# Keeping TensorE's instructions in source order inside the attention heads of a hybrid attention, SSD and retention network

## The chip, the cores and the metric

The kernel runs on one core of one Trainium2 chip. The metric is the device time of one execution in microseconds, and lower is better.

## The reference

Two layers transform 1024 latent tokens and 256 context tokens of width 1024. Each layer normalises the tokens, projects them with one wide matrix, and feeds three mixers that run side by side: differential attention with 4 heads, a bidirectional state-space scan with 16 heads, and bidirectional retention with 4 heads. Their gated outputs are joined and projected back. In the last layer the context tokens serve only as keys and values and as starting states. The part that the change touches is the attention:

```python
def diff_attention(q, k, v, lam):
    s = jnp.einsum('bqhmd,bkhmd->bhmqk', q, k).astype(jnp.float32) * (ATT_QK_DIM ** -0.5)
    p = jax.nn.softmax(s, axis=-1)
    a = p[:, :, 0] - lam * p[:, :, 1]
    return jnp.einsum('bhqk,bkhe->bqhe', a.astype(v.dtype), v)
...
    attn_lat = attn_out(diff_attention_blocked(q_l, jnp.concatenate([k_l, k_c], axis=1),
                                               jnp.concatenate([v_l, v_c], axis=1), lam), ag)
```

Every head has two score maps (m = 0 and 1). The second one's softmax, times lambda, is taken from the first one's, and the difference meets the values. A latent query block of 128 rows sees all 1280 keys; a context query block (first layer only) sees the 256 context keys.

## The kernel before, in words

All dense products are made of three matmuls each, on a split of both factors into a high and a low part (`mm3`, lines 301 to 312). A dense group is 24 such matmuls into one PSUM buffer: L310 with 512 or 256 moving columns (`t_group`: the gates and the output projection), L312 with 256 (`dense_n`, used by `two_units`: queries, keys and values). PSUM has 2 buffers for dense groups (`mm`), 3 for scores (`s`), 2 for transposes (`t`) and 1 for outputs (`o`). Work tiles of SBUF share 8 buffers.

The source is a set of Python generators. `phase(mixer, budget)` walks a mixer, here `head_loop`, step by step; after each step the mixer yields how far it is, and `phase` calls `pump` for dense groups of the stream `dense_all` until the dense work issued reaches that share of the budget. A `two_units` group counts 2.6 and a gates group 5.12 (2.56 with 256 columns). For the heads the budgets are 65, 52, 65, 65 in the first layer and 46, 46, 59, 45 in the second (`SHARE`, line 40, entries 9 to 12). So the source fixes a place for each dense group between steps of a head.

One pass i of `head_loop` (line 1045) in source order is:
- `head_b(i, 0)` (line 979): scores of map 0 of block i, six matmuls (L986) into three `s` buffers, 512, 512 and 256 keys wide; the maximum of each (DVE, L988), their joint maximum `nb` (DVE, L993), and three exponentials with sums (ACT, L998), which give the `s` buffers back
- `head_c1(i-1)`: sums and the factor `rho` of the block before, then `e0 + rho*e1` over 1280 columns (DVE, L1016); first place for dense groups
- `head_c2(i-1)` (line 1020): ten transposes (L149) of that result into three `t` buffers, four, four and two, each copied to SBUF as `aT` (L116 on ACT and L118 on DVE by turns); then `head_a(i+2)` (line 970): four transposes of the split queries `qhl` into one more `t` buffer, copied as `qT`; second place
- `head_b(i, 1)`: scores of map 1, as above; third place
- `head_c3(i-1)` (line 1032): ten products of `aT` with the values (L1037, two matmul records each); then at times one step of `finish_head` of the head before (transposes of `O`) or of `head_prep` of the next one (ten transposes of split keys `khl` for each map); fourth place

The last line of the program that matters here is `TileContext(nc, schedule_with_timeline_sim=True)`. It means that the order of each engine's instructions is not the source's: a planner lays them out before the kernel is run, on a simulated clock. An engine that is free takes, of the instructions that are ready by that clock, the earliest in the source. On the chip every engine then issues its instructions in that fixed order.

Of the kernel before, what the change touches and what calls it, by code (L numbers as in the profile page):

```python
# [47 lines left out]
def drain(g):  # L48
    for _ in g:
        pass  # L50


class Net:
    def __init__(self, tc, ctx, a, outs):
        self.tc, self.nc, self.a, self.outs = tc, tc.nc, a, outs
        ep = ctx.enter_context
        self.act_p = ep(tc.tile_pool(name="act", bufs=1))
        self.w_p = ep(tc.tile_pool(name="wgt", bufs=2))
        self.u_p = ep(tc.tile_pool(name="unit", bufs=NU))
        self.s_p = ep(tc.tile_pool(name="work", bufs=NW))  # L60
        self.c_p = ep(tc.tile_pool(name="const", bufs=1))
        self.t_p = ep(tc.tile_pool(name="tiny", bufs=2))
        self.d_p = ep(tc.tile_pool(name="dram", bufs=1, space=DRAM))
        self.ps_mm = ep(tc.tile_pool(name="ps_mm", bufs=2, space=PSUM))
        self.ps_s = ep(tc.tile_pool(name="ps_s", bufs=3, space=PSUM))
        self.ps_t = ep(tc.tile_pool(name="ps_t", bufs=2, space=PSUM))
        self.ps_o = ep(tc.tile_pool(name="ps_o", bufs=1, space=PSUM))
        self.uid = 0
        self.flip = 0
        self.queue = []  # L70
        self.ready = []
        self.have = {}
        self.ydone = {}
        self.later = []
        self.pieces = []
        self.wu = []
        self.alive = False
        self.x1k = {}
# [1295 lines left out]
    def layer(self, l):  # L1374
        last = l == DEPTH - 1
        cols, cv = self.cc_[l]
        self.mix = self.d_p.tile([16, P, TOK], F32, tag=f"mix{l}", name=f"mix{l}")
        self.x1 = self.d_p.tile([KT, P, TOK], F32, tag=f"x1_{l}", name=f"x1_{l}")
        xin = self.a["xt"] if l == 0 else self.xl
        self.have, self.ydone, self.grp, self.pair, self.heads = {}, {}, {}, {}, {}  # L1380
        self.mixed = False
        self.x1t = {}

        def chain(*gs):
            for i, g in enumerate(gs):
                for f in g:
                    yield (i + (f if f is not None else 0.5)) / len(gs)

        self.first_dense(l, cv, last, self.posts, self.pre)
        self.stream = self.dense_all(l, last, cols, cv, xin)  # L1390
        self.alive = True
        self.phase(chain(self.dt_rest, self.bc_prep(0, last), self.pair_prep(0),
                         self.decay_bufs(), self.g_prep(0, last)), 26)
        share = SHARE[l]
        prep = self.head_prep(0, last)
        for p in range(8):
            def extra(p=p):
                if p == 3:
                    yield from self.bc_prep(1, last)
                    yield from (None for _ in range(4))  # L1400
                if p < 7:
                    yield from self.pair_prep(p + 1)
                else:
                    for _ in range(1):
                        yield next(prep)
            self.phase(self.pair_phase(p, cols, last, extra()), share[p])
        self.post = iter(())
        self.phase(chain(prep), share[8])
        for h in range(4):
            ex = self.head_prep(h + 1, last) if h < 3 else ()  # L1410
            self.phase(self.head_loop(h, last, ex), share[9 + h])
        self.phase(self.ret_mix(0, last), share[13])
        self.phase(self.ret_mix(1, last), share[14])
        drain(self.post)
        self.mixed = True
        while self.alive or self.later:
            self.pump()
        xout = self.outs
        if not last:
            self.xl = xout = self.d_p.tile([KT, P, TOK], F32, tag="xl", name="xl")  # L1420
        self.out2(l, last, cols, xout)
# [132 lines left out]
```

## Time and profile before

| what | value |
|---|---|
| median of 3 runs | 2871.17 us (2867.28 to 2872.06) |
| the profiled execution | 2869.1 us |
| its span, first to last instruction | 2867.3 us |
| TensorE (PE) busy | 2665.5 us, 93% of the span |
| VectorE (DVE) busy | 1781.3 us, 62% |
| ScalarE (ACT) busy | 1056.4 us, 37% |
| mean granted TensorE clock | 0.964 of full speed |

The time of a run is that of the program on the device; the span leaves out 1.8 us before the first and after the last instruction. TensorE has a row for matmuls (PE) and one for weight loads (PEld) that overlaps it. The ends of matmuls are modelled, so that PE counts as busy for some 0.16 us after the last matmul of a chain has been issued and passed.

### The profile page before, as it was taken

The page shows a single profiled execution, that of the slowest core. Times are in us where ns is not written, and L with a number is a line of the kernel's source. Part 1 is how long each engine was busy: PE and PEld are TensorE (multiplying, and loading weights), DVE is VectorE, ACT ScalarE, POOL GpSimd, SP SyncE. Part 2 cuts the span into 40 slices and gives each one's busy share as a digit, 9 for nine tenths or more (in the row PEclk, how much of TensorE's full clock was granted, in tenths as well). Part 3 has the DMA queues.
Part 4 walks back from the last instruction along what each step waited for, and adds up shares of the span by engine and source line. Part 5 has one row for each costly group of instructions (what it writes and reads, how often), then busy time and mean ns, then how long its engine had stood idle before and what let it go on. Part 6 is the DMA issues. An engine that isn't in the chain of part 4 may idle for free.

```text
span 2867.3 us, 45100 instructions
## 1 busy us (share of the span) xinstructions
PE 2665.5 (93%) x17116; PEld 2339.0 (82%) x17116; DVE 1781.3 (62%) x4213; ACT 1056.4 (37%) x2678; POOL 772.1 (27%) x688
## 2 busy tenths in 40 slices
PE   6799999999999999989989989999999999999999
PEld 4578877888888899977878777878988888889787
DVE  5567767656677766565435566667676767564651
ACT  3443333224454545341223443332254444442330
POOL 2333223232111121243331423223421221022540
PEclk9899999999999999998999999999999999999999
DMA  6021212222111111033452112112210010002461
GB/s 244 10 62 62 67 44 83 70 69 89 45 54 45 54 31 39 27 110 109 136 179 95 36 41 72 53 50 65 60 30 16 23 30 23 23 17 66 139 209 55
DMA packets 111832, 196.04 MB, mean 68 GB/s; under 512 B 13600, under 2 KB 43104, under 8 KB 111616
## 3 DMA queue, kind: packets, MB, share of 16 engines
q1 hardware_dynamic: 111616, 193.17, 21.3%
q8 instruction: 135, 2.21, 0.3%
q14 instruction: 81, 0.66, 0.1%
HBM read 155.43 MB, written 37.68 MB: 67 GB/s over the span
## 4 chain that ended last, share of the span: by engine, by line
PE 76%; DVE 12%; ACT 3%; issue 2%; DMA 2%; POOL 1%; SPq 0%; DVEq 0%; ACTq 0%; POOLq 0%
PE mm L310 34%; PE mm L312 18%; PE t L149 5%; PE o L1037 4%; PE s L986 4%; PE s L772 2%; PE s L822 2%; DVE mx L988 2%; PE o L815 2%; PE t L793 1%; ACT e L998 1%; DVE e L1016 1%; DMA mr<-mix 1%; DVE rs L1156 1%; PE s L1146 1%
## 5 line engine op out<-in xcount | busy, mean ns | idle before, releaser
L310 PE MATMUL mm<-ah,wh 128*128 128x512 f32 (+1 forms) x1680 | 629.4, 375 | 30.1 <-DVE xr L1223 13.8
L310 PE MATMUL mm<-al,wh 128*128 128x512 f32 (+1 forms) x1680 | 622.8, 371 | 1.5 <-DVE al L284 0.9
L310 PE MATMUL mm<-ah,wl 128*128 128x512 f32 (+1 forms) x1680 | 622.4, 371 | 0.6 <-POOL wl L284 0.6
L284 POOL TENSOR_TENSOR wl<-raw,wh 128x512 fp32r<-128x512 f32 x224 | 294.5, 1335 | 769.5 <-ACT wh L282 736.9
L312 PE MATMUL mm<-wh,ah 128*128 128x256 f32 x1568 | 455.7, 291 | 9.5 <-DVE q L118 7.0
L312 PE MATMUL mm<-wl,ah 128*128 128x256 f32 x1568 | 450.4, 287 | 0.0
L312 PE MATMUL mm<-wh,al 128*128 128x256 f32 x1568 | 448.7, 286 | 0.0
L310 PEld LDWEIGHTS mm<-ah,wh 128*128 128x128 f32 x1680 | 322.3, 192 | 85.8 <-issue 13.8
L310 PEld LDWEIGHTS mm<-al,wh 128*128 128x128 f32 x1680 | 322.2, 192 | 51.1 <-issue 1.4
L310 PEld LDWEIGHTS mm<-ah,wl 128*128 128x128 f32 x1680 | 321.2, 191 | 51.2 <-POOL wl L284 1.1
L312 PEld LDWEIGHTS mm<-wh,ah 128*128 128x128 f32 x1568 | 302.5, 193 | 16.6 <-DVE q L118 7.7
L998 ACT ACTIVATE e<-s,nb 128x512 f32<-128x512 f32 (+1 forms) x384 | 231.7, 613 | 206.2 <-DVE nb L993 203.6
L312 PEld LDWEIGHTS mm<-wl,ah 128*128 128x128 f32 x1568 | 302.7, 193 | 2.4 <-POOL wl L284 0.2
L312 PEld LDWEIGHTS mm<-wh,al 128*128 128x128 f32 x1568 | 302.3, 193 | 2.2 <-issue 0.2
L988 DVE TENSOR_REDUCE mx<-s 128x1 f32<-128x512 f32 (+1 forms) x400 | 225.1, 589 | 55.4 <-PE s L986 53.2
L986 PE MATMUL s<-kT,qT 128*128 128x512 f32 (+1 forms) x800 | 215.8, 375 | 17.0 <-ACT e L998 15.5
L282 ACT ACTIVATE wh<-raw 128x512 fp32r<-128x512 f32 x224 | 130.0, 625 | 226.2 <-PE mm L310 103.9
L1037 PE MATMUL o<-v,aT 128*128 128x128 f32 x1312 | 174.9, 276 | 0.0
L986 PEld LDWEIGHTS s<-kT,qT 128*128 128x128 f32 x800 | 134.3, 193 | 41.3 <-ACT e L998 26.5
L1037 PEld LDWEIGHTS o<-v,aT 128*128 128x128 f32 x1312 | 163.8, 193 | 4.1 <-DVE v L118 0.8
L794 ACT ACTIVATE t<-t 128x512 f32<-128x512 f32 x144 | 82.2, 582 | 146.5 <-PE t L793 142.5
L766 POOL TENSOR_TENSOR xw<-xn,dtpk 128x512 f32<-128x512 f32 (+2 forms) x96 | 79.4, 838 | 208.9 <-PE s L772 93.5
(282 smaller groups left out, 4544.5 us busy)
## 6 DMA issues: line engine op xcount, KB each, us to landing
raw<-in_wi_dram SPq DMA_DIRECT2D x176, 256.0 KB
wa<-in_wa_dram SPq DMA_DIRECT2D x48, 512.0 KB
E<-cume SPq DMA_DIRECT2D x144, 128.0 KB
mr<-mix SPq DMA_DIRECT2D x64, 256.0 KB
raw<-in_wo_dram SPq DMA_DIRECT2D x32, 256.0 KB
x<-xr SPq DMA_DIRECT2D x26, 256.0 KB
mix<-cv SPq DMA_DIRECT2D x8, 640.0 KB
mix<-sg SPq DMA_DIRECT2D x8, 640.0 KB
```

The lines of the kernel that those rows point to most:

```text
L149: self.nc.tensor.transpose(ps[:, j * P:(j + 1) * P], srcs[i + j], self.ident)
L282: nc.scalar.activation(out=hi, in_=x, func=AF.Copy)
L284: e.tensor_tensor(out=lo, in0=x, in1=hi.bitcast(F32), op=ALU.subtract)
L310: nc.tensor.matmul(ps, lhsT=w, rhs=x, start=st, stop=sp)
L312: nc.tensor.matmul(ps, lhsT=x, rhs=w, start=st, stop=sp)
L766: nc.gpsimd.tensor_tensor(out=xw, in0=xn[:, a:a + m].rearrange("p t (h e) -> p t h e", h=2), in1=self.wend[:, a:a + m, h0:h0 + 2].unsqueez ...
L772: nc.tensor.matmul(ps[:, j * P:(j + 1) * P], lhsT=bn[:, c, :], rhs=xw[:, j].rearrange("p h e -> p (h e)"), start=True, stop=True)
L794: nc.scalar.activation(out=ps, in_=ps, func=AF.Exp)
L986: nc.tensor.matmul(ps[:, 0:n], lhsT=qT[:, 2 * m + s, :], rhs=kT[m][:, t0:t0 + n], start=(s == 0), stop=(s == 1))
L988: nc.vector.tensor_reduce(out=mx[:, ci:ci + 1], in_=ps[:, 0:n], axis=AX.X, op=ALU.max, negate=len(chunks) == 1)
L998: nc.scalar.activation(out=em[:, t0:t0 + n], in_=pss[ci][:, 0:n], func=AF.Exp, bias=nb, accum_out=z[:, 3 * m + ci:3 * m + ci + 1])
L1037: nc.tensor.matmul(po[:, 0:P], lhsT=aT[j], rhs=v[:, j, :], start=(j == b0), stop=(j == NT - 1))
```

## The change

A thin wrapper `Ordered` stands in front of TensorE. While its flag `pin` is set, each matmul or transpose that is traced gets an edge that keeps it, in the planner's order, behind the instruction traced just before it on TensorE. The edge sets the order of issue and no wait. The flag is set in `layer` around the four `head_loop` phases, with all the dense groups that `phase` pumps into them. `Core` passes the other engines through as they were.

```diff
+class Ordered:
+
+    def __init__(self, tc, tensor):
+        self.tc, self.tensor, self.pin = tc, tensor, False
+
+    def kept(self, ins):
+        if self.pin:
+            self.tc.keep_in_program_order(ins)
+        return ins
+
+    def matmul(self, *a, **k):
+        return self.kept(self.tensor.matmul(*a, **k))
+
+    def transpose(self, *a, **k):
+        return self.kept(self.tensor.transpose(*a, **k))
+
+
+class Core:
+    def __init__(self, tc):
+        self.tensor = Ordered(tc, tc.nc.tensor)
+        for x in ("vector", "scalar", "gpsimd", "sync"):
+            setattr(self, x, getattr(tc.nc, x))
...
-        self.tc, self.nc, self.a, self.outs = tc, tc.nc, a, outs
+        self.tc, self.nc, self.a, self.outs = tc, Core(tc), a, outs
...
             ex = self.head_prep(h + 1, last) if h < 3 else ()
+            self.nc.tensor.pin = True
             self.phase(self.head_loop(h, last, ex), share[9 + h])
+            self.nc.tensor.pin = False
```

## Rows read from the trace of the kernel before

**Rows 1.** The page, busy time of each engine over the span.
```profile
PE 2665.5 (93%) x17116; PEld 2339.0 (82%) x17116; DVE 1781.3 (62%) x4213; ACT 1056.4 (37%) x2678; POOL 772.1 (27%) x688
```

**Rows 2.** Busy time in the head stretches of both layers; then clock, DMA share.
```profile
635.00:1180.00 545.00, 520.20 (x3789) 471.79 (x3789) 373.76 (x895) 253.40 (x773) 97.67 (x64) 0.99 0.15 47
2085.00:2580.00 495.00, 458.77 (x3263) 422.31 (x3262) 342.08 (x812) 229.24 (x691) 93.17 (x66) 0.98 0.08 24
```

**Rows 3.** What TensorE waited for, 635 to 1180: total us, times, longest.
```profile
PE s L986 <- ACT e L998: 7.6, 7, 2.2
PE t L149 <- DVE khl L284: 6.1, 5, 2.7
```

**Rows 4.** The same, 2085 to 2580.
```profile
PE s L986 <- ACT e L998: 7.9, 8, 2.2
PE t L149 <- DVE khl L284: 5.0, 5, 2.9
```

**Rows 5.** Timeline of TensorE from 641.5: start, us, engine, line, operation.
```profile
641.64 0.63 PE L986 MATMUL s<-kT,qT 128*128 128x512 f32 x2
642.11 0.28 PE L312 MATMUL mm<-wh,ah 128*128 128x256 f32 x1
...
642.57 0.62 PE L986 MATMUL s<-kT,qT 128*128 128x512 f32 x2
```

**Rows 6.** Timeline of TensorE from 2361; idle before and its releaser in brackets.
```profile
2362.52 1.06 PE L149 MATMUL t<-ident,e 128*128 128x128 f32 x8 [0.50 <-DVE e L1016]
2364.33 0.44 PE L149 MATMUL t<-ident,e 128*128 128x128 f32 x2 [0.75 <-ACT aT L116]
2367.19 0.45 PE L149 MATMUL t<-ident,qhl 128*128 128x128 f32 x1 [2.43 <-DVE nb L993]
...
2379.69 1.82 PE L986 MATMUL s<-kT,qT 128*128 128x512 f32 x4 [2.19 <-ACT e L998]
```

**Rows 7.** Windows of 10 us around it; the clock follows POOL.
```profile
2350.00:2360.00 10.00, 10.00 (x78) 9.54 (x78) 5.99 (x13) 7.03 (x21) 6.51 (x6) 1.00 0.32 87
2360.00:2370.00 10.00, 6.32 (x41) 5.71 (x41) 7.77 (x14) 2.81 (x8) 1.02 (x1) 0.84 0.07 19
```

**Rows 8.** Timeline from 853, all engines.
```profile
853.50 1.07 PE L149 MATMUL t<-ident,khl 128*128 128x128 f32 x8 [2.74 <-DVE khl L284]
...
854.17 0.60 ACT L116 ACTIVATE kT<-t 128x512 fp32r<-128x512 f32 x1 [1.31 <-PE t L149]
854.61 0.69 DVE L118 CAST kT<-t 128x512 fp32r<-128x512 f32 x1 [0.65 <-PE t L149]
...
854.82 0.69 PE L149 MATMUL t<-ident,khl 128*128 128x128 f32 x2 [0.25 <-ACT kT L116]
...
855.35 1.12 PE L149 MATMUL t<-ident,e 128*128 128x128 f32 x4
```

**Rows 9.** Groups by line, 635 to 1180: count, busy us, mean ns of one.
```profile
L988 DVE TENSOR_REDUCE mx<-s 128x1 f32<-128x512 f32 (+1 forms) x208 | 116.0, 583 | 30.5 <-PE s L986 29.3 <-ACT e L998 0.3
L1016 DVE SCALAR_TENSOR_TENSOR e<-e,rho,e 128x1280 f32<-128x1280 f32 (+1 forms) x40 | 57.6, 1441 | 0.8
L993 DVE TENSOR_REDUCE nb<-mx 128x1 f32<-128x3 f32 x64 | 9.8, 153 | 0.9
L998 ACT ACTIVATE e<-s,nb 128x512 f32<-128x512 f32 (+1 forms) x192 | 115.8, 613 | 106.1 <-DVE nb L993 103.8 <-PE t L149 1.9
L998 ACT ACTIVATION_READ_ACCUMULATOR e<-s,nb 128x1 f32 x192 | 38.6, 201 | 0.0
```

**Rows 10.** Long pieces of the chain that ended last: start, us, what.
```profile
104.44 11.10 PE mm L310 x48
...
2443.55 8.63 PE mm L312 x72
```

**Rows 11.** Timeline of TensorE from 858.2.
```profile
858.94 2.40 PE L1037 MATMUL o<-v,aT 128*128 128x128 f32 x20
...
861.99 0.94 PE L986 MATMUL s<-kT,qT 128*128 128x512 f32 x4
```

## The prediction

> **What bounds the kernel now.** I read the page first, for the engine that sets the end. TensorE is busy for 93% of the span, VectorE for 62% [rows 1], so the end moves with the time in which TensorE waits or runs slowly. Next come the windows of the two head stretches, 1040 us together. TensorE is busy for 520.2 and 458.8 us of them and idle for 61.0 us, VectorE is busy for 69% and ScalarE for 46%, and the granted clock is 0.99 and 0.98 [rows 2]. [...]
>
> Then the list of waits in each stretch tells what ends those idle times: 15.5 us of scores that wait for exponentials to free a score buffer, and 11.1 us of key transposes that wait for the split `khl` [rows 3, 4]. The rest is spread over many short waits. The timeline shows how the planner's order works. Where dense work is at hand, a pair of scores stands between single matmuls of a dense group [rows 5]: each step of a head comes just when the planner thinks that its input is ready, and dense matmuls fill what is between. Where the planner placed no dense work, TensorE stops between the steps of a head, for 2.43 and 2.19 us [rows 6], and the clock falls to 0.84 in that window of 10 us, after 1.00 in the one before [rows 7].
>
> **The change, part by part.** No operation is added or dropped; the wrapper is gone by the time the program runs. What changes is TensorE's order in the heads, and, by the planner's clock, the orders that VectorE, ScalarE and GpSimd take behind it. In source order the six scores of a map stand together, so do the fourteen transposes of `head_c2` and `head_a`, the twenty products, and each dense group. So three things move.
>
> *Waits that go away.* The key transposes keep their place behind the products of a block and their splits; I leave their 11.1 us as they are. That leaves 61 - 11 = 50 us of idle that belongs to the planner's order. A wait is longer than the view shows, since a matmul of 256 columns is shown as 0.28 us long [rows 5] while 72 of them follow each other in 8.63 us, 0.12 each [rows 10]: the last 0.16 us before a wait count as busy. The four kinds of rows 3 and 4 make 26.6 us in 25 waits, 1.06 us each; at that mean the 50 us are some 47 waits, and 47 x 0.16 is 8. I take away 58 us.
>
> *A wait that comes with the source order.* The transposes have two buffers. Source order asks for 4, 4, 2 and again 4 transposes without anything between. The trace has one such run, 4, 4 and 2 of `khl` and then 4 of `e` [rows 8]: TensorE starts at 853.50, ScalarE's copy of the first buffer ends at 854.77, the third group starts at 854.82, VectorE's copy of the second ends at 855.30, and the fourth starts at 855.35. These 1.85 us hold ten transposes, which take 0.114 us each ((1.07 - 0.16) / 8 in the same rows), so 1.14; 0.71 us is lost. Without the fourth group it is 1.32 - 8 x 0.114 = 0.41. Today the planner mostly puts dense matmuls or scores into these gaps; the pinned order can't. There are 64 blocks with all keys (8 in each of 4 heads and 2 layers), and 48 of them have a `head_a` behind (7 per head in the first layer, where ten blocks run, 5 in the second). That makes 48 x 0.71 + 16 x 0.41 = 41 us. Both copies ran there as soon as they could. That is the lower bound; the upper one is the run where the third group waited for a visible 0.75 us after eight transposes [rows 6], three times the 0.25 of rows 8, about 0.5 more for each block, 73 us. A copy finds VectorE busy in 69% of cases, with half an operation of 0.4 us to go, and ScalarE in 46%, and few other things compete at that point, so I stay near the lower bound and add 0.1 us for each block: 47 us.
>
> *Chains that source order leaves too little room for.* From the start of a map's scores a chain runs to the first free score buffer: 0.62 for two scores [rows 5], three maxima at 0.58, `nb` 0.15, one exponential with its sum 0.61 + 0.20: 3.3 us. All three exponentials end at 4.95 us, and with three tiny steps (taken like `nb`) and the combination at 1.44 the transposes can begin at 6.85 us [rows 9]. Against that stands the work that source order puts between. A dense group takes 24 x 0.12 = 2.9 us with 256 columns, 24 x 0.23 = 5.55 with 512 [rows 10]; six scores at these rates 1.2, the products 2.4 [rows 11], fourteen transposes 1.6. A pass of the first layer gets 65 / 11 = 5.9 of its budget, two groups of 2.6 or about one of 5.12, so most passes have dense work in two of their four places: 1.2 + 2.9 + 2.4 + 1.2 + 2.9 = 10.6 us between the scores of map 1 and the transposes that need them, and 3.75 to spare. I walked the loop with its budgets through both layers. Between the scores of the two maps nine places have no dense group and 2.8 us (0.5 short each, 4.5 in all), and once two sets of scores stand side by side (2.1 short); between the scores of map 1 and the transposes ten places have less than 6.85 (2.4 once, 5.2 twice, 5.9, 6.5 twice, 6.7 three times, and one just met; 10 us short). The sum is 16.5 us. A TensorE that waits for one of them gives room to the next, down to 5 us in all; one more us of queue in front of VectorE lifts it to 41. I take 20, as VectorE has free time in 31% of the stretch. At the start of each of eight heads, scores follow two groups of query transposes and wait for a copy of about 0.7 us: 6 us (bounds 3 and 8).
>
> *Sum.* New waits 47 + 20 + 6 = 73, less 58: 15 us longer. The profiled execution took 2869.1 us, 2.1 below the median of the runs shown, so 2884 there and 2886 as a median. The bounds: 41 + 5 + 3 - 58 = -9 and 73 + 41 + 8 - 58 = +64 us.
>
> TensorE's queue holds everything behind a waiting instruction, so a wait for a copy also holds back the next scores and, one step on, VectorE's maxima. No DMA is moved past another by the pins, which act on TensorE alone; a dense group that runs later asks for its weights later, and GpSimd, which splits them, is busy for 18% of the stretch [rows 2].
>
> On the clock, the stretch after the long waits had 0.84 [rows 7]. [...]
>
> **The rivals.** *Faster: slack beats the planner's timing.* The planner leaves a head's step no time to spare, and pays where its clock is wrong or its dense work has been spent, as in rows 6. Source order spreads dense groups evenly and leaves 3 to 4 us in most chains. [...] It decides when less than about 0.8 us for each block is lost in all. Against it speaks that 41 of today's 58 us come back for certain, by two buffers.
>
> *Nothing to measure.* The same terms cancel: 58 out, 52 to 64 in. 2871. By the sum, 15 us decide between this and the forecast, less than the bounds of one term.
>
> *Much slower: queues in front of VectorE.* If VectorE's planned order doesn't suit and each copy and each chain meets a queue, the terms are at their upper bounds: +45 to +64 us, 2925. Against it: it has 31% free time.
>
> [...]
>
> **How the numbers follow.** Forecast (+6 to +45) 0.40, faster 0.30, no change 0.18, much slower by queues 0.08 and by the clock 0.04. A measurement can tell 0.2%, 5.7 us, from no change. So faster 0.30, same 0.18, slower 0.52. The range from 2842 to 2926 leaves out the far ends of the first and the last two cases, about 0.07 below and 0.10 above; it holds both signs. The forecast's own range is 2877 to 2916.
>
> **What would show it.** In the profile after: six scores, twenty products and fourteen transposes each in one piece; transposes of `e` and `qhl` that wait for `aT` copies, for 0.25 us and more, in most blocks (new: some 15 to 30 us in the list of waits); scores that wait for exponentials only where no dense group stands between; no clusters of 2 us without dense work; the clock at 0.98 or above. The prediction is wrong if waits for `aT` stay under 10 us in all, if the idle time of the two stretches falls below 45 us, or if the time moves outside the heads.

## The result, and the profile after

The changed kernel takes 3045.43 us (median of 4 runs, 3039.06 to 3047.56), against 2870.86 for the kernel before beside it. The ratio is 1.0608, with a 95% interval from 1.059 to 1.0625. It is 175 us slower. The forecast was 15 us longer, and the range ended at 2926.

The page of the changed kernel, span and busy time of each engine [rows 1]:
```profile
span 3041.5 us, 45101 instructions
...
PE 2731.6 (90%) x17116; PEld 2370.8 (78%) x17116; DVE 1789.0 (59%) x4213; ACT 1068.6 (35%) x2678; POOL 767.4 (25%) x688
```
The instruction counts are the same on every engine. TensorE's busy time has grown by 66 us with the same 17116 matmuls, so part of the loss isn't waiting. The windows of its two head stretches, in the columns of [rows 2]:
```profile
630.00:1286.00 656.00, 567.74 (x3830) 499.44 (x3830) 372.18 (x886) 259.00 (x770) 94.08 (x64) 0.93 0.12 39
2193.00:2734.00 541.00, 469.10 (x3140) 420.17 (x3141) 339.68 (x788) 230.67 (x683) 89.02 (x63) 0.95 0.07 22
```
From the first scores to the last products the stretches were 541.5 and 485.9 us long and are now 655.7 and 539.9 (the windows have small margins), so 168 of the 175 us are here. (They don't hold quite the same work: the first has some 70 matmuls more, which stood ahead of it before the change, and begins 5 us earlier; the second has some 50 fewer.) TensorE's idle time in them has grown from 61.0 us to (656 - 567.74) + (541 - 469.10) = 160.2 us, and its busy time from 979 to 1037 us. The granted clock has fallen from 0.99 and 0.98 to 0.93 and 0.95. Taken in windows of half a us, it is 1.00 in 2064 of the 2394 windows of the two stretches, 0.50 in 279 and between the two in 51; before the change, 2002, 62 and 16 of 2080. With these two levels, an estimate is 2 x 0.07 x 656 + 2 x 0.05 x 541 = 146 us at 0.50, after 31 by the same reckoning; with a clock of two digits such sums are good to some 10 us. The 115 us more cost at most half of that, 57 us. VectorE's share fell to 57 and 63%, so it is not the bound.

Outside the heads there is one smaller effect. The windows after the last head, first of the changed kernel, then of the one before:
```profile
2734.00:3042.00 308.00, 295.68 (x1654) 256.34 (x1652) 139.65 (x274) 70.74 (x178) 100.37 (x100) 0.99 0.34 109
```
```profile
2571.00:2868.00 297.00, 285.45 (x1582) 245.98 (x1580) 140.70 (x274) 69.36 (x176) 101.50 (x102) 0.99 0.35 113
```
There are 72 matmuls more in the tail, three dense groups of 24. The free order had placed them earlier, most of them in the last heads. The tail is 11 us longer.

What TensorE waited for in the first stretch (total us, times, longest), which answers to [rows 3]:
```profile
PE t L67 <- ACT qhl L306: 20.9, 25, 2.3
PE t L67 <- DVE qhl L308: 17.3, 19, 4.2
PE t L67 <- DVE nb L1017: 7.4, 7, 2.7
PE t L67 <- DVE e L1040: 7.4, 6, 3.2
PE t L64 <- DVE adar L142: 7.2, 6, 3.0
PE t L67 <- ACT aT L140: 7.0, 11, 0.7
PE t L67 <- DVE aT L142: 6.6, 15, 1.3
...
PE s L64 <- ACT e L1022: 2.6, 1, 2.6
```
and in the second one [rows 4]:
```profile
PE t L67 <- ACT qhl L306: 27.9, 22, 2.1
PE t L67 <- DVE qhl L308: 14.3, 11, 4.1
PE t L67 <- DVE aT L142: 10.2, 20, 1.0
PE t L67 <- ACT aT L140: 7.9, 10, 2.2
```
The scores that waited for exponentials are nearly gone (15.5 us before), and the key transposes no longer wait for `khl` at all. The waits for the copies `aT` make 31.7 us, just above the 15 to 30 foreseen for the list. On top stands a wait that no term of the sum has: query transposes that wait for their own input, the split `qhl`, in 77 places for 80.4 us. (All of TensorE's instructions pass through the wrapper and so have its lines, L64 for matmuls and L67 for transposes. L306 and L308 are the high and the low half of a split, L140 and L142 copies, L1022 the exponentials, L1040 the combination. Where the list names `nb`, L1017, another operation of VectorE had ended 0.06 to 0.07 us before, with `nb` right behind it: in seven of these waits, 4.7 us, a copy `aT`, in two, 5.1 us, the combination, and in one, 5.1 us, `adar`.)

One pass of the changed kernel, from its timeline (start, us, engine, line, operation; idle before and its releaser in brackets):
```profile
850.24 1.03 PE L67 MATMUL t<-ident,e 128*128 128x128 f32 x8
...
850.43 0.28 ACT L140 ACTIVATE q<-mm 128x128 f32<-128x128 f32 x1 [3.65 <-PE mm L64]
...
851.37 0.60 ACT L140 ACTIVATE aT<-t 128x512 f32<-128x512 f32 x1 [0.66 <-PE t L67]
...
852.02 0.44 PE L67 MATMUL t<-ident,e 128*128 128x128 f32 x2 [0.75 <-ACT aT L140]
852.03 1.01 DVE L142 COPY aT<-t 128x512 f32<-128x512 f32 x2
852.15 0.69 ACT L1022 ACTIVATE e<-s,nb 128x512 f32<-128x512 f32 x1 [0.18 <-DVE nb L1017]
...
853.49 0.47 ACT L1022 ACTIVATE e<-s,nb 128x256 f32<-128x256 f32 x1
...
853.94 0.42 ACT L306 ACTIVATE qhl<-q 128x256 fp32r<-128x256 f32 x1
854.39 0.77 DVE L308 TENSOR_TENSOR qhl<-q,qhl 128x256 fp32r<-128x256 f32 x1 [1.34 <-ACT qhl L306]
854.41 0.33 PE L67 MATMUL t<-ident,qhl 128*128 128x128 f32 x1 [1.95 <-ACT qhl L306]
...
855.22 0.55 PE L67 MATMUL t<-ident,qhl 128*128 128x128 f32 x3 [0.48 <-DVE qhl L308]
855.52 0.64 PE L64 MATMUL s<-kT,qT 128*128 128x512 f32 x1
```
The fourteen transposes take 1.6 us of work, and here stand for 5.3 us. ScalarE copies `aT`, then does three exponentials, and only then splits `qhl`, though it had stood idle for 3.65 us before 850.43. VectorE's low half follows the high one, and TensorE meets both as it gets there. The scores behind them, whose buffers the exponentials had given back by 853.96, start only at 855.52. The same piece of a pass in the kernel before, from its timeline:
```profile
798.16 1.03 PE L149 MATMUL t<-ident,e 128*128 128x128 f32 x8
798.95 0.36 PE L312 MATMUL mm<-wh,ah 128*128 128x256 f32 x1
...
802.01 0.41 ACT L282 ACTIVATE qhl<-q 128x256 fp32r<-128x256 f32 x1
...
802.23 0.38 PE L149 MATMUL t<-ident,e 128*128 128x128 f32 x2
...
803.69 0.42 DVE L284 TENSOR_TENSOR qhl<-q,qhl 128x256 fp32r<-128x256 f32 x1
...
805.18 0.28 PE L149 MATMUL t<-ident,qhl 128*128 128x128 f32 x1
```
There, too, the split comes late: it starts 3.9 us after the first transposes of `e`, and in the changed kernel 3.7. But dense matmuls, scores and products stand between, and TensorE does not stop between 798 and 807 us. What the change took away is this filling.

The low clock stands at such places. The windows of 10 us around the pass, to be set beside [rows 7]:
```profile
840.00:850.00 10.00, 10.00 (x82) 9.73 (x81) 8.96 (x28) 4.19 (x13) 0.00 (x0) 1.00 0.01 2
850.00:860.00 10.00, 6.82 (x39) 5.78 (x38) 7.19 (x16) 3.68 (x10) 5.47 (x3) 0.83 0.00 0
860.00:870.00 10.00, 8.66 (x68) 7.95 (x67) 7.46 (x19) 6.34 (x20) 0.00 (x0) 1.00 0.01 2
```
The six scores behind the waits, from 855.52 to 857.67, take 2.15 us at a granted clock of 0.54; the next six, from 863.89 to 865.06, take 1.17 us at 1.00. So work behind the waits ran slower as well.

### The profile page after: what moved, and what is told of

Read it like the earlier page. It is cut to its first block, busy times and chain, and to the rows that moved or that the text cites. A ratio compares the mean times of both kernels' runs of the same rounds, so it can differ in the third digit from the quotient of the medians.

```text
span 3041.5 us, 45101 instructions
## 1 busy us (share of the span) xinstructions
PE 2731.6 (90%) x17116; PEld 2370.8 (78%) x17116; DVE 1789.0 (59%) x4213; ACT 1068.6 (35%) x2678; POOL 767.4 (25%) x688
## 4 chain that ended last, share of the span: by engine, by line
PE 70%; DVE 15%; ACT 5%; issue 3%; DMA 2%; POOL 1%; SPq 0%; DVEq 0%; ACTq 0%; POOLq 0%
PE mm L64 48%; PE s L64 9%; PE o L64 6%; PE t L67 5%; DVE mx L1012 2%; ACT e L1022 2%; PE t L64 2%; DVE e L1040 1%; DVE aT L142 1%; DVE qhl L308 1%; POOL wl L308 1%; DMA mr<-mix 1%; DVE rs L1180 1%; DVE cv L536 1%; ACT wh L306 1%
## 5 line engine op out<-in xcount | busy, mean ns | idle before, releaser
L64 PE MATMUL mm<-ah,wh 128*128 128x512 f32 (+1 forms) x1680 | 634.0, 378 | 32.9 <-DVE xr L1247 15.4
L64 PE MATMUL mm<-al,wh 128*128 128x512 f32 (+1 forms) x1680 | 626.7, 373 | 1.5 <-DVE al L308 0.9
L64 PE MATMUL mm<-ah,wl 128*128 128x512 f32 (+1 forms) x1680 | 624.7, 372 | 0.6 <-POOL wl L308 0.6
L308 POOL TENSOR_TENSOR wl<-raw,wh 128x512 fp32r<-128x512 f32 x224 | 296.7, 1346 | 1125.7 <-ACT wh L306 1106.7
L64 PE MATMUL mm<-wh,ah 128*128 128x256 f32 x1568 | 457.7, 292 | 7.8 <-DVE q L142 5.7
L64 PE MATMUL mm<-wl,ah 128*128 128x256 f32 x1568 | 450.9, 288 | 0.2 <-POOL wl L308 0.2
L64 PE MATMUL mm<-wh,al 128*128 128x256 f32 x1568 | 449.8, 287 | 0.0
L64 PEld LDWEIGHTS mm<-ah,wh 128*128 128x128 f32 x1680 | 326.1, 194 | 87.8 <-issue 15.7
L64 PEld LDWEIGHTS mm<-al,wh 128*128 128x128 f32 x1680 | 325.9, 194 | 52.1 <-issue 1.4
L64 PEld LDWEIGHTS mm<-ah,wl 128*128 128x128 f32 x1680 | 324.6, 193 | 52.8 <-POOL wl L308 1.1
L64 PEld LDWEIGHTS mm<-wh,ah 128*128 128x128 f32 x1568 | 307.3, 196 | 10.1 <-DVE q L142 5.9
L1022 ACT ACTIVATE e<-s,nb 128x512 f32<-128x512 f32 (+1 forms) x384 | 232.2, 614 | 223.7 <-DVE nb L1017 222.7
L64 PEld LDWEIGHTS mm<-wl,ah 128*128 128x128 f32 x1568 | 307.3, 196 | 0.5 <-POOL wl L308 0.4
L64 PEld LDWEIGHTS mm<-wh,al 128*128 128x128 f32 x1568 | 306.5, 195 | 0.3 <-issue 0.2
L306 ACT ACTIVATE wh<-raw 128x512 fp32r<-128x512 f32 x224 | 130.1, 626 | 235.0 <-PE mm L64 113.1
L64 PE MATMUL s<-kT,qT 128*128 128x512 f32 (+1 forms) x800 | 203.2, 390 | 3.1 <-ACT e L1022 3.1
L64 PEld LDWEIGHTS s<-kT,qT 128*128 128x128 f32 x800 | 152.8, 206 | 33.3 <-ACT e L1022 8.5
L64 PE MATMUL o<-v,aT 128*128 128x128 f32 x1312 | 159.0, 276 | 0.0
L64 PEld LDWEIGHTS o<-v,aT 128*128 128x128 f32 x1312 | 153.9, 193 | 0.5
L67 PE MATMUL t<-ident,e 128*128 128x128 f32 x656 | 103.5, 290 | 51.5 <-DVE aT L142 16.9
L67 PE MATMUL t<-ident,qhl 128*128 128x128 f32 x288 | 68.4, 334 | 89.0 <-ACT qhl L306 53.2
```

What stands on the lines that cost most here:

```text
L64: return self.kept(self.tensor.matmul(*a, **k))
L67: return self.kept(self.tensor.transpose(*a, **k))
L306: nc.scalar.activation(out=hi, in_=x, func=AF.Copy)
L308: e.tensor_tensor(out=lo, in0=x, in1=hi.bitcast(F32), op=ALU.subtract)
L1022: nc.scalar.activation(out=em[:, t0:t0 + n], in_=pss[ci][:, 0:n], func=AF.Exp, bias=nb, accum_out=z[:, 3 * m + ci:3 * m + ci + 1])
```

## The experiments

Theory 1: the split of the queries is late. Source order takes work tiles (8 shared buffers) for the copies `aT` first and for `qhl` after them, and the split's place on ScalarE follows from it. Rivals: the transposes' two buffers (2), dense groups that can't move into gaps (3), and, as a guess at the cause of the low clock, the runs of transposes.

**Early split.** The changed kernel, with the split (its tile too) put ahead of the pass's first scores; the transposes stay where they were. At the start of a head two splits still stand right before their transposes.
```diff
+    def head_s(self, q, i):
         hl = self.work("qhl", (P, 2, 2, 2, 64), F32R)
...
+        return hl
+
+    def head_a(self, hl):
...
+                if i + 2 < nq:
+                    hl = self.head_s(q, i + 2)
                 e0 = self.head_b(qTs[i], kT, 0, z, ch[i])
...
-                qTs[i + 2] = self.head_a(q, i + 2)
+                qTs[i + 2] = self.head_a(hl)
```


> The changed kernel with the query split moved: its tile is taken and written at the head of the pass, before the scores of map 0, and its four transposes stay where they were. Theory 1 (the split is late, because work tiles are taken in source order and the split's tile comes after the three tiles of the copies, so that TensorE in source order meets it unready): the waits for qhl, 80 us in the heads, fall below 15 us, some 30 us of low clock go with them, and the time falls from 3045 to 2935 to 2975 us. Theory 2 (two transpose buffers): the copies of the transposes were the limit all along and the split only came last; the wait moves to the copies and the time stays above 3015 us.

It took 2970.84 us, ratio 1.0339 (1.0322 to 1.0355), 75 us less than the changed kernel. The waits of its first stretch:
```profile
PE t L67 <- DVE e L1043: 17.4, 10, 3.2
PE t L64 <- DVE adar L142: 12.5, 7, 5.4
PE t L67 <- DVE aT L142: 9.0, 16, 1.9
PE t L67 <- ACT aT L140: 7.9, 13, 0.8
PE t L67 <- DVE qhl L308: 5.7, 2, 3.3
```
The waits for `qhl` are down from 84.8 to 21.7 us in the whole run (17.2 in the two stretches, where less than 15 was expected), and others have grown in part. The 13 that are left all stand at the starts of heads. So the late split inside the passes is 75 of the 175 us.

**Own tile.** The changed kernel, with `qhl` in a buffer of its own (and 7 shared ones), the source order unchanged.
```diff
-        hl = self.work("qhl", (P, 2, 2, 2, 64), F32R)
+        hl = self.s_p.tile([P, 2, 2, 2, 64], F32R, tag="qhl", name=self.nm("qhl"), bufs=1)
```


> The changed kernel with the query split in a tile of its own (one buffer) and seven work buffers in place of eight, so that the count of buffers is the same. The place in the source is as in the changed kernel. Theory 1 (the order in which tiles are taken holds the split back): the split is planned before the copies and the time is 2935 to 2985 us. Rival (ScalarE simply has no time for the split before the copies): qhl waits stay at 60 us or more, time above 3020 us.

2970.66 us in one run, the same as with the early split, and the waits for `qhl` are down to 23.4 us. It is the place in the row of shared buffers that held the split back, not its place in the source.

**Early split, free order.** The kernel before with the early split and no pins.

> The kernel before, without any pin, with the query split moved to the head of the pass as in split_early. If the late split costs only where TensorE may not pass it (theory 1): 2855 to 2880 us, no more than 15 us from the kernel before. If the late split is a cost of its own whatever the order: below 2830 us.

2862.14 us, ratio 0.9968 (0.9953 to 0.9983). Where the order is free, the late split cost nearly nothing, because it was covered.

**Heads only.** The changed kernel, with the head's steps chained among themselves and the dense groups free to move between them.
```diff
+        keep = self.nc.tensor.pin
+        self.nc.tensor.pin = False
         try:
             return next(self.stream)
...
+        finally:
+            self.nc.tensor.pin = keep
```


> The steps of the heads keep source order among themselves, but the dense groups that are pumped between them stay free to be moved and cut up. Theory 3 (what costs is that no dense matmul can stand in a gap any more): waits in the heads fall back to the 61 us of before and the time to 2865 to 2900 us, with the split as late as ever. Theory 1b (the order among the head's own steps costs, since each waits for the one before): time above 2950 us.

2977.97 us, ratio 1.0364 (1.0343 to 1.0386). Dense groups that may move bring back 67 of the 175 us, more than half is still lost, and so the theory that their fixed places are the whole cause fell. The windows of its head stretches:
```profile
637.00:1237.00 600.00, 547.06 (x3767) 486.06 (x3766) 367.14 (x886) 255.09 (x768) 92.56 (x63) 0.95 0.13 43
2146.00:2685.00 539.00, 476.02 (x3187) 431.61 (x3186) 330.70 (x787) 229.02 (x684) 90.08 (x60) 0.93 0.07 22
```
The first layer's stretch is 57 us shorter than with all pinned, the second one's only 1 us. Its clock is even lower, at 0.93, and the waits for the combination have grown to 45.0 us in the whole run, in 22 places.

**Second layer only.** Pins in the last layer alone (`pin = last`).

> The pins in the second layer alone. The profile of the changed kernel puts 109 us of the loss before the end of the first layer's heads, 54 us in the second layer's heads and 11 us behind them. If the two layers' losses are their own: 2925 to 2945 us. If the first layer's late end shifted the second one's weights or buffers: below 2910 us.

2934.54 us in one run: the two layers' losses add up, as the first layer was as long as before.

**Modulation free.** The early split, with the groups of the modulation matrix (`adar`, a product and eight small transposes of its copy) taken out of the pins, since TensorE waited for that copy for 12.5 us.

> split_early, with the matmuls and small transposes of the modulation groups (ada, seven of them in the first layer's heads) left out of the pins, and the other pinned instructions chained to each other. In split_early these seven cost 12.5 us of waits for their row copy. If they are a cost by themselves with the low clock behind them: 2940 to 2958 us against 2971. If the first layer's loss is elsewhere: above 2963 us.

2971.36 us in one run, no gain, as its rival had it. The waits for `adar` fell to 7.9 us in the first stretch and others took their place: a wait in the list is not a price.

**Apart.** As the last one, with the transposes taken apart in the source: eight of `e`, the second dense place, the last two, the scores of map 1, and then the four of the queries.
```diff
-                aT = self.head_c2(e[0], ch[j])
-            if i + 2 < nq:
-                qTs[i + 2] = self.head_a(hl)
+                aT, rest = self.head_c2(e[0], ch[j])
             yield (i + 0.5) / (nq + 1)
+            if j >= 0:
+                rest()
             if i < nq:
                 e1 = self.head_b(qTs.pop(i), kT, 1, z, ch[i])
                 st[i] = ((e0, e1), z)
+            if i + 2 < nq:
+                qTs[i + 2] = self.head_a(hl)
```


> ada_free, with the fourteen transposes taken apart in the source: the first eight of head_c2, then a place for dense groups, then the last two, then the scores of map 1, then the four query transposes. If the two transpose buffers cost what the waits for aT say (39 us in split_early, 7 before): those waits fall below 12 us and the time by 25 to 45 us against ada_free, to 2900 to 2930 us. If these waits hide behind others: less than 12 us gained.

2923.7 us, ratio 1.0177 (1.0158 to 1.0195), 47.7 us less than with the modulation free. Its windows:
```profile
635.00:1235.00 600.00, 548.32 (x3835) 493.89 (x3834) 366.66 (x889) 257.79 (x770) 93.44 (x64) 0.95 0.13 43
2144.00:2623.00 479.00, 443.87 (x3144) 405.72 (x3143) 334.99 (x784) 229.87 (x684) 88.19 (x60) 0.99 0.08 24
```
The time came out as expected, and a little better. That the two buffers are the whole of it is not shown: in the two stretches the waits for `aT` fell from 40.5 to 23.9 us, where less than 12 was expected, the idle time from 111 to 87, and the edit also gives the query transposes a later place and the dense groups another one. The clock moved little: it is 0.95 and 0.98 with the early split, where the fourteen transposes stand in one piece, and 0.95 and 0.99 here.

The second layer's stretch, from first scores to last products, is 478.2 us, against 485.9 before the change. It holds some 50 matmuls fewer, though, and the tail behind it is 10 us longer (306.5 us, after 296.7). Both together are as long as before, within 2 us, in a fixed order.

**Apart, heads only.** The same with the dense groups free, by the edit of the run "heads only".

> The early split with the transposes taken apart, with pins on the head's own steps alone: the dense groups of the stream are free. What is left of the loss there (2924 us) sits in the first layer, whose stretch is 599 us against 542 before, while the second layer's is already as short as before. Theory (short chains: the source's places for dense groups leave too little work behind the scores in some passes): with the dense groups free the first layer falls below 575, the waits for exponentials and combinations below 12 us, and the time to 2885 to 2905 us. Rival (the head's own order costs, dense places don't matter): the first layer stays above 590 and the time above 2915. Second rival: free dense groups move to where they are ready first and leave the second layer's chains bare, as they did when the heads alone were pinned without the other two edits (538.6 us): the second layer grows above 500, and the time ends near 2924 again.

2888.54 us, ratio 1.0059 (1.004 to 1.0077), 35 us less. Its windows:
```profile
634.00:1188.00 554.00, 524.31 (x3777) 474.06 (x3776) 369.33 (x886) 253.50 (x767) 93.22 (x64) 0.98 0.14 47
2097.00:2596.00 499.00, 459.30 (x3210) 421.75 (x3210) 324.99 (x788) 228.52 (x687) 85.63 (x60) 0.97 0.08 23
```
The first layer's clock is back at 0.98 and its stretch at 554 us, 60 matmuls lighter. The second layer's grew by 20 us, but has some 60 matmuls more, and the tail is 15 us shorter (291.2): both together grew by 4 us, so the second rival did not come true. Free dense groups pay in the first layer. That short chains are the reason isn't shown: the waits for exponentials and combinations there fell only from 22.8 to 17.0 us, not below the 12 expected, and those for `qhl` (6.8 us) and `adar` (5.4) went as well.

**Apart, free order.** The kernel before with both edits and no pins.

> The kernel before with the early split and with the transposes taken apart in the source, without pins. Theory 1 (source order matters only where it is kept; the planner moves the steps anyway): within 8 us of the early split alone, 2854 to 2870 us. Rival (the source order of transposes is good by itself, since it sets priorities): below 2850.

2859.58 us, ratio 0.9959 (0.9946 to 0.9971): with a free order it hardly matters where the source puts the transposes.

**Fill.** The changed kernel, with four spare matmuls of 512 columns, whose result nobody reads, just before the query transposes of a pass.
```diff
             if i + 2 < nq:
+                ps = self.pmm()
+                for _ in range(4):
+                    self.nc.tensor.matmul(ps, lhsT=qTs[i][:, 0, :], rhs=kT[0][:, 0:512], start=True, stop=True)
                 qTs[i + 2] = self.head_a(q, i + 2)
```


> The changed kernel with four more matmuls of 512 columns just before the four query transposes of a pass; they need only what the scores of the pass needed, and nothing reads their result. 56 places x 4 x 0.23 us = 52 us of added TensorE work at full speed, put where the late split makes TensorE wait. Theory A (the low clock follows the waits): the work fills what were visible waits for qhl (80 us in all, now below 30) and the hidden 0.16 us of each, the granted clock of the head stretches rises from 0.93 and 0.95 to 0.96 or more, and the time falls in spite of the added work, to 2995 to 3030 us. Theory B (the low clock comes from runs of transposes, or from dense work that stands elsewhere): waits fall as above, but the clock stays where it is, and the time stays at 3040 to 3075. Theory C (waits are queues that only move on): 3075 to 3100.

3023.36 us, ratio 1.0528 (1.0507 to 1.0548). With 52 us of added work the kernel is 22 us faster. Its windows:
```profile
631.00:1280.00 649.00, 578.64 (x3964) 511.94 (x3964) 370.69 (x889) 259.19 (x771) 93.83 (x64) 0.96 0.12 40
2187.00:2717.00 530.00, 475.31 (x3235) 424.25 (x3236) 339.54 (x788) 230.47 (x683) 88.99 (x63) 0.98 0.08 22
```
The idle time is 125 us in place of 160, and the time at the lower level 2 x 0.04 x 649 + 2 x 0.02 x 530 = 73 us in place of 146, with as many transposes in the same order. The waits for `qhl` fell to 46.3 us, less than expected (below 30). Time and clock came out as theory A has it. By itself this run doesn't exclude theory B, since the spare matmuls also stand in the middle of each run of fourteen transposes. The early split and "apart" do that: in the second layer the clock rose to 0.98 with these runs as they were, and taking them apart moved it by 0.01 at most. Nor does the sum of the waits alone set the clock. By the same reckoning the stretches of "heads only" have 116 us of idle time and 135 us at the lower level, those of "fill" 125 and 73. Whether the length of single waits decides, how close they stand, or what runs between them, stays open.

**Fill, free order.** The same four matmuls in the kernel before.

> The control: the same added matmuls in the kernel before, without pins. The planner can put them where TensorE is idle (61 us in the head stretches), but most will stand beside other work: 52 us of work, so 2900 to 2925 us by all theories; less than 2890 would mean that there, too, filling idle time brings back more than it costs.

2891.22 us, ratio 1.0068 (1.0047 to 1.0089). All theories had expected 2900 to 2925. The 52 us of work cost 18: the free order could put part of it where TensorE was idle, and its stretches have 37 us of idle time, after 61.

**Mixed.** Pins in the second layer alone, with "apart" there, and the early split in both layers.

> Early split in both layers; in the second layer pinned with the transposes taken apart and the modulation groups free, in the first layer the order free. If the layers are additive (as the run with pins in the second layer alone says), the second layer gives its 478 us against 484 of the free one, so 5 us under the early split alone: 2850 to 2862 us. If the tail, which came out 11 us longer behind pinned heads, is lost as well: 2862 to 2875.

2864.92 us, ratio 0.997 (0.9958 to 0.9983), no better than the free order with the same edits. The windows of its last heads and tail:
```profile
2081.00:2562.00 481.00, 443.44 (x3138) 404.71 (x3138) 335.43 (x783) 229.35 (x682) 87.25 (x59) 0.99 0.08 24
2562.00:2868.00 306.00, 295.49 (x1656) 256.18 (x1655) 142.46 (x278) 70.81 (x178) 102.32 (x104) 0.99 0.34 110
```
The heads are as short as in "apart", but the tail has 74 matmuls more than before the change, which dense groups in fixed places leave over, and is 9 us longer. The second expectation held. The two versions with a free order, 2859.6 and 2862.1 us, stay the fastest.

## Why the prediction was wrong

The direction was the likeliest one, the size was off by a factor of more than ten. One way through the runs splits the loss into 74.6 us for the late split (3045.4 to 2970.8), 47.7 for the transposes in one piece (2971.4 to 2923.7), 35.2 for dense groups in fixed places (to 2888.5) and 29.0 for the order of the head's own steps (to 2859.6), less the 11.3 us by which the two edits beat the kernel before in a free order. That such a chain adds up to the whole (175.2, where 174.6 were measured) is no proof, since each step begins about where the last one ended. The sizes depend on the order of the steps: dense groups set free first, with the late split in place, brought 67 us. (The medians of the kernel before beside these runs lay between 2870 and 2873.)

*The step that failed* is "A wait that comes with the source order". It lets the four query transposes wait only for a transpose buffer, and takes the time of a fourth group from a run in which that group was of `e`, whose data had long been there [rows 8]. The query transposes have an input of their own, the split `qhl`. The prediction never asked when it is ready, as the list of waits shows hardly any wait for it before the change. It was late there too, and covered. What the runs showed in its place: 80.4 us of waits for `qhl` in 77 places, and 75 us less time when the split comes earlier, by either of two edits.

The same input was overlooked at the starts of heads. There the sum has 6 us, for scores that wait for the copy `qT`. The list after the change has no such wait; the 13 waits for `qhl` that the early split leaves, 21.7 us, stand there.

One row was also misread. Where query transposes followed those of `e` with nothing between, TensorE stood still for 2.43 us [rows 6], which the prediction took for a place without dense work. Rows of the same trace tell another reason:
```profile
2364.17 0.41 ACT L282 ACTIVATE qhl<-q 128x256 fp32r<-128x256 f32 x1
...
2366.36 0.68 DVE L118 COPY aT<-t 128x512 f32<-128x512 f32 x1
...
2367.36 0.42 DVE L284 TENSOR_TENSOR qhl<-q,qhl 128x256 fp32r<-128x256 f32 x1
```
The high half, which the first of these transposes reads, was there at 2364.58. But VectorE's copy out of the second transpose buffer stood behind other operations and ended only at 2367.04; the transpose came at 2367.19. So the term for two buffers had a dearer example than the 0.75 us that it took for its upper bound.

Had this one step been right, the forecast would still have failed. With the early split the kernel is 100 us slower than before, against 15 forecast. TensorE's busy time is then 41 us above that before (2706.9 and 2665.5 us), its idle time in the stretches 57 us (118 and 61), and the time at the lower clock 52 us (83 and 31, which costs at most 26). The sum has no term for the clock.

*The clock* had a chance of 0.04, and fell to 0.93 and 0.95. Runs of transposes alone did not bring this. The second stretch of the early split has the same runs of fourteen transposes, with fewer waits:
```profile
2170.00:2666.00 496.00, 449.44 (x3141) 406.22 (x3141) 334.15 (x789) 230.14 (x683) 90.41 (x63) 0.98 0.08 23
```
The clock is 0.98 there, as before the change, and rose in "fill" to 0.96 and 0.98 without a transpose moved. Whether such runs have a part in it beside the waits is not shown. The prediction had seen the low clock, 0.84, behind a long wait [rows 7], and could have given each of its new waits such a price: 100 us more of idle time came with 115 us more at the lower level, though the run "heads only" shows that the two don't keep step. The share of the clock in the 175 us is only bounded, at 57 us or less.

*Waits that go away* (58 us): two kinds did, scores that waited for exponentials (15.5 us before, 3.1 after) and the 11.1 us for `khl`, which the sum had left standing. For the rest it isn't shown. Of the 160 us of idle time after the change, 48 by the list belong neither to `qhl` nor to `aT`, and the list can't tell which of them are old.

*Two transpose buffers* (47 us, bounds 41 and 73): the waits for `aT` are 31.7 us in 56 places after the change, 40.7 with the 0.16 us of each that counts as busy. Taking the transposes apart brought 47.7 us, but other things moved with them, so that these numbers agree so closely is in part luck. The mechanism is seen in the list, and the size is about right.

*Short chains* (20 us, bounds 5 and 41): 9.9 us of waits for the combination (15.0 with the two under `nb`) and 3.1 for exponentials in the whole run after the change; the waits for the late split may have given these chains room, for with the early split they are 21.5 and 8.0 us. By the list these sizes lie within the bounds. The 46 us that free dense groups brought in the first layer (600 to 554) hold more than chains, as said above, and are no measure of this term.

*Rivals.* The faster case needed less than 0.8 us lost for each block; the waits for `qhl` and `aT` alone came to 112 us for 64 blocks. Nothing shows that queues in front of VectorE decided, as the rival had it: in the list the waits for `aT` stay near the forecast. But no run tried them alone; VectorE's smaller share only says that the same work fills a longer stretch. In the list of what would show it, six scores and twenty products in one piece came as foreseen, as did the waits for `aT` (31.7 us, just above the 15 to 30); clusters without dense work stayed, and the clock did not stay at 0.98. None of the three signs of being wrong came up: waits for `aT` are above 10 us, the idle time is above 45, and nearly all of the time moved inside the heads.

## What to carry to other kernels

Before an engine is given a fixed order, ask of each step when each of its inputs is ready, from the timeline of the producers; a list of waits names only those that nothing covered, and free order can hide a late producer (in the pass shown, a split that starts 3.9 us after the first transposes). Buffers taken in turn from a shared row tie a producer to the ones ahead of it: put a small, early result in a tile of its own or write it early (here 75 us by either). Give a set of new waits a price for the clock too (here it fell from 0.99 and 0.98 to 0.93 and 0.95), and don't take a wait in the list for the time that its removal brings: 63 us less of waits for `qhl` brought 75, 4.6 us less for `adar` nothing.

## What the runs showed of the hardware

Added work made the kernel faster: 52 us of matmuls that nobody needs (224, at 0.23 us each by [rows 10]) took 22 us off; idle time fell by 35 us, and the time at the lower level of the clock, as estimated from two levels, from 146 to 73 us. In the changed kernel the level fell behind the 0.75, 1.95 and 0.48 us of waits of the pass shown (clock 0.83 in that window of 10 us), and was back at 1.00 in the next one, although that has waits of 0.69 and 0.65 us. In the two stretches, with 0.93 and 0.95, the waits for `qhl` and `aT` last 0.84 us on average (112.1 us in 133 places).
